# Residual rows turned on VectorE, x's features in a permuted order, decay's sums one piece later, vectors in one load

## The chip, the cores and the metric

The kernel runs on one core of one Trainium2 chip. The metric is the device time of one execution in microseconds. The times before are 1664.04, 1663.55 and 1665.42 us; their median is 1664.04 us.

## The reference

A hybrid of a Conformer layer and an mLSTM layer over 256 latent tokens (x) with a context prefix of 256 tokens (ctx), 1024 features, batch 1. All is fp32. Each sub-layer computes x <- LN(ALPHA*x + gate * F(x*(1+scale)+shift)), where scale, shift and gate come from a conditioning vector (adaLN). Cut to what matters here:

```python
for i in range(DEPTH):                       # DEPTH = 2
    sh1, sc1, g1, sh2, sc2, g2 = adaln(c, ada_w[i], ada_b[i])
    u = modulate(h, sh1, sc1)
    # layer 0: y = conformer_conv(u, ...); layer 1: y = mlstm_mixer(u, uc, ...)
    h = layer_norm(ALPHA * h + g1 * y, ln1_g[i], ln1_b[i])
    h = layer_norm(ALPHA * h + g2 * sq_relu_mlp(modulate(h, sh2, sc2), mlp_w1[i], mlp_w2[i]), ln2_g[i], ln2_b[i])
    # layer 0 does the same for the context tokens

# in the mLSTM: gates -> decay
lf = jax.nn.log_sigmoid(f_pre)
bcum = jnp.cumsum(lfc, axis=-1)              # running sums of the log forget gates, per head and direction
dlog = bcum[..., :, None] - bcum[..., None, :] + ic[..., None, :]
o = jax.nn.sigmoid(xm @ w_o + b_o)           # output gates
```

## The kernel before

The hidden state lies with features on the partitions: x is eight tiles of 128 features by 512 tokens (256 of the context, LO, then 256 latent, HI). A matrix product in fp32 is three passes of TensorE: each operand is split into a rounded high part (a cast by ScalarE, line 151) and a low rest (a subtraction by VectorE, line 152), and the products high-high, high-low and low-high add up in PSUM (`mm3`, lines 182 to 186, and `mm3t`, lines 213 to 215, where the roles of weights and data are exchanged). Weights come as 1 MB loads on SyncE's queue (`raw_load`, line 145, three buffers), and are split into `wh` and `wl`, four buffers each.

The order on each engine is not the order of the text alone. The framework's planner places each instruction when its inputs are due by its own costs; the place in the text decides between those that are due. `tc.issue_after` queues an instruction behind another one of its engine.

Stages that the change touches:

- The start. `vecs` holds all small vectors, 408 columns on 128 partitions. The first 64 columns (the two conditioning vectors and layer 0's adaLN bias) are loaded ahead of everything else (line 117), the other 344 after the loads of the second feature block (line 657). Then `start0` and `start1` run over eight feature blocks: one adaLN weight load, a load of x, a load of pw1 weights, matmuls (line 344).
- Between the products up_z and up_x of layer 1. The layer's input is also wanted as rows (tokens on the partitions) for the residual sum of layer 1. Eight ScalarE instructions (line 1199) scale the latent half of x; TensorE turns it in 16 transposes of 128x128 into PSUM (line 1202), ScalarE copies the result into the tile R (line 1204) and stores it to the DRAM tile `r_dr` (line 1205).
- The gate stage. Main work and side work are two chains of generators. The table `att` says which: first `['o0', 'G0 W0 T0 W1', 2]`, i.e. the output gates of head 0 (`gate_o`) with the side pieces `decay`, `weights(0)`, `guards`, `weights(1)`, two side pieces after each main piece; then `['o1', 'A0 W2', 1.6]`, and so on. A main piece of `gate_o` is 12 matmuls 512 wide; a head has 16 of them, eight for each direction d, and after each direction two adds read the sums out of PSUM (og, line 1588). `decay` brings the gates into columns (line 1398), takes log sigmoid (lines 1412 to 1421, two of them on ScalarE: Exp and Ln), makes running sums by matmuls with a triangle (lines 1435 and 1436, "decay's sums"), turns the result (line 1443), scans it and stores the negated row maxima `negm` to DRAM (`ng_dr`, line 1451). `weights(h)` loads rows of `ng_dr` spread over all partitions (line 1510) and builds the decay matrices from them on ScalarE and VectorE.
- The load of R from `r_dr` (line 1573), written ahead of the second half of head 0's gates, behind the latest weight load. R is first used by `down(0)`, beside the gates of head 2.

The tile R and the tiles that turn v (line 1261, VectorE transposes in 32x32 blocks, stored in four pieces at line 1265) share one buffer, "res".

Of the kernel before, what the change touches and what calls it, by code (L numbers as in the profile page):

```python
# [14 lines left out]
P = 128  # L15
D = 1024
DT = D // P
# [4 lines left out]
C = 256  # L22
# [34 lines left out]
_OFF = {}  # L57
# [14 lines left out]
def hybrid_kernel(ctx: ExitStack, tc: tile.TileContext, xT, vecs_d, wdw_d, ada0_w, ada_w, wg_d, pw1a, pw1, pw2, w1_0, w2_0,  # L72
                  w1_1, w2_1, up_x, up_z, wv, wo, bo_d, wk, wq, wqT, wdown, rows_d, out):
    nc = tc.nc
# [10 lines left out]
    def nm(s):  # L85
        uid[0] += 1
        return f"{s}_{uid[0]}"
# [3 lines left out]
    def tmp(tag, dt=F32):  # L91
        return tp.tile([P, T], dt, tag=tag, name=nm(tag), bufs={"E": 4, "S": 2, "L": 2, "F": 1}[tag])
# [8 lines left out]
    def psum(tag="mm"):  # L101
        return pp.tile([P, 512], F32, tag=tag, name=nm(tag), bufs={"mm": 3, "ln": 2, "fl": 1, "cv": 2}[tag])
# [10 lines left out]


    vecs = con.tile([P, NV], F32, name="vecs")
    NV0 = _OFF["ada_b1"][0]
    nc.sync.dma_start(vecs[:, :NV0], vecs_d[:, :NV0])

    def V(name, i=0, n=1):
        o = _OFF[name][0]  # L120
# [2 lines left out]
    def VA(name):  # L123
        o, w = _OFF[name]
        return vecs[:, o:o + w]

    ident = con.tile([P, P], F32, name="ident")
# [484 lines left out]
    x, u = [], []  # L612
# [41 lines left out]
    start1(0)  # L654
    idle(spare, 5)
    start0(1)
    nc.sync.dma_start(vecs[:, NV0:], vecs_d[:, NV0:])
    for f in range(DT):
        start2(f, (0,))
        if f + 1 < DT:  # L660
# [295 lines left out]
    cv = [psum("cv") for _ in range(2)]  # L956
# [234 lines left out]
    def rows_tile():  # L1191
        return xp.tile([P, 2, D], F32, tag="res", name=nm("res"), bufs=1)

    r_dr = dp.tile([P, 2, D], F32, name="r_dr")
    R = rows_tile()
    for f in range(0, DT, 2):
        t, tr = tmp("S"), psum("cv")
        for i in range(2):
            nc.scalar.activation(t[:, i * C:(i + 1) * C], x[f + i][:, HI], AF.Identity, scale=al[:, 0, f + i:f + i + 1],
                                 bias=al[:, 1, f + i:f + i + 1])  # L1200
            for tt in range(2):
                nc.tensor.transpose(tr[:, tt * C + i * P:tt * C + (i + 1) * P],
                                    t[:, i * C + tt * P:i * C + (tt + 1) * P], ident)
        nc.scalar.copy(R[:, :, f * P:(f + 2) * P], tr.rearrange("p (t c) -> p t c", t=2))
    nc.scalar.dma_start(r_dr, R)

    xm = []

# [99 lines left out]
    S = {}  # L1308
# [83 lines left out]
    def decay(_):  # L1392
        gT = tmp("L")
        nc.scalar.copy(gT, gps)
        yield
        gk = psum("ln")
        for b in range(4):
            nc.tensor.matmul(gk[:, b * 16:(b + 1) * 16], gT[:, b * P:(b + 1) * P], foldg, start=True, stop=True)
        gs = tmp("S")[:, 0:64].rearrange("p (b c) -> p b c", b=4)
        nc.vector.tensor_tensor(gs, gk[:, 0:64].rearrange("p (b c) -> p b c", b=4),  # L1400
                                VA("b_gate").rearrange("p (b c) -> p b c", b=4), op=ALU.add)
        gb_ = [tmp("L"), tmp("E"), tmp("E")]
        g8 = [gb_[i // 3][:, (i % 3) * 4 * NG:(i % 3 + 1) * 4 * NG].rearrange("p (b c) -> p b c", b=4) for i in range(8)]
        ig, fg, bsb, ex, up1, cor, lf, fa = g8
        nc.vector.memset(ig, 0.0)
        nc.vector.memset(fg, 0.0)
        for d in range(2):
            nc.vector.tensor_copy(ig[:, :, 32 * d:32 * d + 4], gs[:, :, 8 * d:8 * d + 4])
            nc.vector.tensor_copy(fg[:, :, 32 * d:32 * d + 4], gs[:, :, 8 * d + 4:8 * d + 8])


        nc.vector.scalar_tensor_tensor(fa, fg, -1.0, fg, op0=ALU.mult, op1=ALU.max)
        nc.scalar.activation(ex, fa, AF.Exp, scale=-1.0)
        nc.vector.tensor_scalar(up1, ex, 1.0, None, op0=ALU.add)
        nc.vector.scalar_tensor_tensor(cor, up1, -1.0, ex, op0=ALU.add, op1=ALU.subtract)
        nc.scalar.activation(lf, up1, AF.Ln)
        nc.vector.reciprocal(up1, up1)
        nc.vector.tensor_tensor(cor, cor, up1, op=ALU.mult)
        nc.vector.tensor_tensor(lf, cor, lf, op=ALU.subtract)
        nc.vector.tensor_scalar(fa, fg, 0.0, None, op0=ALU.min)  # L1420
        nc.vector.tensor_tensor(lf, lf, fa, op=ALU.add)

        nc.vector.memset(up1, 0.0)
        for d, (b0, b1, b2, b3) in ((0, (0, 1, 2, 3)), (1, (1, 0, 3, 2))):
            c = slice(32 * d, 32 if d == 0 else NG)
            nc.vector.tensor_copy(up1[:, b1, c], lf[:, b0, c])
            nc.vector.tensor_tensor(up1[:, b2, c], up1[:, b1, c], lf[:, b1, c], op=ALU.add)
            nc.vector.tensor_tensor(up1[:, b3, c], up1[:, b2, c], lf[:, b2, c], op=ALU.add)
        yield
        yield  # L1430
        bps = psum("ln")
        for d, cum in ((0, upper), (1, lower)):
            c = slice(32 * d, 32 if d == 0 else NG)
            reg = bps[:, 0:4 * NG].rearrange("p (b c) -> p b c", b=4)[:, :, c]
            nc.tensor.matmul(reg, cum, lf[:, :, c], start=True, stop=False)
            nc.tensor.matmul(reg, ones, up1[:, :, c], start=False, stop=True)
        nc.vector.tensor_copy(bsb, bps[:, 0:4 * NG].rearrange("p (b c) -> p b c", b=4))
        nc.vector.tensor_tensor(acol, ig, bsb, op=ALU.subtract)

        yield  # L1440
        aT = psum("ln")
        for b in range(4):
            nc.tensor.transpose(aT[:NG, b * P:(b + 1) * P], acol[:, b, :], ident)
        aR, mR = tmp("S"), tmp("S")
        nc.vector.tensor_copy(aR[:32, :], aT[:32, :])
        nc.vector.tensor_copy(aR[32:NG, LO], aT[32:NG, LO])
        nc.vector.tensor_copy(aR[32:NG, HI], aT[32:NG, T - 1:C - 1:-1])
        nc.vector.tensor_tensor_scan(mR[:NG, :], aR[:NG, :], aR[:NG, :], 0.0, op0=ALU.max, op1=ALU.max)
        nc.vector.tensor_scalar(negm[:32, :], mR[:32, HI], -1.0, None, op0=ALU.mult)
        nc.vector.tensor_scalar(negm[32:NG, :], mR[32:NG, T - 1:C - 1:-1], -1.0, None, op0=ALU.mult)  # L1450
        nc.scalar.dma_start(ng_dr, negm)
        bsbs.append(bsb)
        yield
# [42 lines left out]
    G1 = rows(qe.tile([P, D], F32, name="G1"), rows_d[0:1])  # L1496
    R = rows_tile()
    for i in range(2):
# [59 lines left out]
    for i in range(2):  # L1558
        rx = raw_load(xl_dr[i].rearrange("p b c -> p (b c)"))
        for j in range(8):  # L1560
            t = XL(F32R)
# [4 lines left out]
    def gate_o(h):  # L1566

        for d in range(2):
            bo = rows(BO().rearrange("p a b -> p (a b)"), bo_d[h:h + 1, d * DH:(d + 1) * DH])
            pss = [psum() for _ in range(2)]  # L1570
            if (h, d) == (0, 1):
                with tc.issue_after(loaded[0]):
                    nc.sync.dma_start(R, r_dr)
            for q in range(4):
                ws = preo if (h, d, q) == (0, 0, 0) else None
                if ws is None:
                    raw = raw_load(wo[h, d, q])
                for i in range(2):
                    w = ws[i] if ws else split_w(raw[:, i * 1024:(i + 1) * 1024])
                    for t in range(2):  # L1580
                        for k in range(2):
                            kt = 4 * q + 2 * i + k
                            sl = slice(k * 512, (k + 1) * 512)
                            mm3t(pss[t], xls[kt][0][:, BLK[t]], xls[kt][1][:, BLK[t]], w[0][:, sl], w[1][:, sl],
                                 kt == 0, kt == ET - 1)
                        if q == 3 and i == 1:
                            og[h, d, t] = o_ = OG()
                            nc.vector.tensor_tensor(o_, pss[t], bo, op=ALU.add)  # L1588
                            nc.scalar.activation(o_, o_, AF.Sigmoid)
                    yield  # L1590
# [73 lines left out]
    def down(h):  # L1664
# [18 lines left out]
        if h == 0:  # L1683
            for hf, ws in enumerate(load()):
                for t in range(2):
# [3 lines left out]
                    nc.vector.tensor_tensor(e_, ps, G1[:, HF[hf]], op=ALU.mult)  # L1689
                    nc.vector.tensor_tensor(R[:, t, HF[hf]], R[:, t, HF[hf]], e_, op=ALU.add)  # L1690
                    yield
# [28 lines left out]
    def residual(t, hf, ps, G):  # L1720

        e_ = tmp("E")
        nc.vector.tensor_tensor(e_, ps, G[:, HF[hf]], op=ALU.mult)
        nc.vector.tensor_tensor(R[:, t, HF[hf]], R[:, t, HF[hf]], e_, op=ALU.add)
        if hf == 0:
# [240 lines left out]
def _layout(np, i):  # L1966
    g = {k: np.asarray(v) for k, v in i.items()}
    a, turned = {}, _turned(np)
    a["xT"] = np.concatenate([g["ctx"][0], g["x"][0]], axis=0).T
    vec = {  # L1970
        "c_ctx": _cols(g["c_ctx"]), "c": _cols(g["c"][0]),
        "b_pw1": _cols(g["conv_b_pw1"][0]),
# [32 lines left out]
    a["wqT"] = g["ml_w_q"][0].T.reshape(ET, P, E)  # L2005
    a["wdown"] = g["ml_w_down"][0].reshape(H, 4, P, 2, 512).transpose(0, 3, 2, 1, 4).reshape(H, 2, P, 2048)
    a["w2_1"] = g["mlp_w2"][1].reshape(16, 2, P, D).transpose(0, 2, 1, 3).reshape(16, P, 2048)
    ab = g["ada_b"][1].reshape(6, D)
    a["rows_d"] = np.stack([ab[2], ab[5], g["ln1_g"][1], g["ln1_b"][1], g["ln2_g"][1], g["ln2_b"][1]])
    return {k: np.ascontiguousarray(v) for k, v in a.items()}  # L2010

# [22 lines left out]
```

## Time and profile before

| | |
|---|---|
| median of 3 runs | 1664.04 us (1663.55 to 1665.42) |
| profiled execution, own time | 1665.14 us |
| its span, first to last instruction | 1663.4 us |
| TensorE busy | 1648.7 us, 99% |
| VectorE busy | 1038.1 us, 62% |
| ScalarE busy | 734.6 us, 44% |
| DMA | 303.70 MB, mean 183 GB/s |
| granted TensorE clock | 0.999 |

The profile is of one execution on the chip. PE is TensorE's matmuls, PEld its weight loads, DVE is VectorE, ACT ScalarE, POOL GpSimd, SP SyncE; ACTq and SPq are rows of the queues that issue DMAs. A row of a timeline has start and duration in us, engine, line, operation, output <- input, shape and count, and in brackets the idle time of the engine ahead of it with what ended it. A row of a line has minimum, median and maximum duration in ns.

### The profile page before, as it was taken

What the parts mean: (1) busy time and instruction counts of PE and PEld (TensorE: products, weight loads), DVE (VectorE), ACT (ScalarE), POOL (GpSimd) and SP (SyncE); (2) the same over time, 40 slices, a digit from 0 to 9 for tenths busy, and PEclk for the clock granted to TensorE, in tenths of its full rate; (3) what the DMA queues carried; (4) which work ended last, traced back from release to release, by engine and by line L of the source; (5) the groups of instructions that cost most, each with busy time, mean ns of one, the idle gap of its engine ahead of it and who ended that gap; (6) DMA issues with size and microseconds to landing.
All of it is one profiled execution on the core that took longest, in us unless ns stands there. A gap on an engine that the chain in (4) does not pass through costs nothing.

```text
span 1663.4 us, 22731 instructions
## 1 busy us (share of the span) xinstructions
PE 1648.7 (99%) x8856; PEld 1357.6 (82%) x8856; DVE 1038.1 (62%) x1863; ACT 734.6 (44%) x1182; POOL 14.4 (1%) x64
## 2 busy tenths in 40 slices
PE   9999999999999999999999999999999999999998
PEld 6665898888888998877787899888877888878886
DVE  6554895666535765762354753553489876776677
ACT  4313573232324476652233533442477654555453
POOL 0000000000000000000000000000000000000001
PEclk9999999999999999999999999999999999999999
DMA  9555223534324065557774852554465555675552
GB/s 353 208 210 214 92 75 111 167 123 148 136 101 152 4 228 194 184 196 266 278 259 146 302 179 79 179 194 144 148 240 197 203 215 203 250 284 183 178 194 85
DMA packets 74331, 303.70 MB, mean 183 GB/s; under 512 B 7694, under 2 KB 23858, under 8 KB 44144
## 3 DMA queue, kind: packets, MB, share of 16 engines
q1 hardware_dynamic: 56368, 286.49, 49.1%
q10 hardware_dynamic: 17856, 15.77, 2.8%
q8 instruction: 69, 1.13, 0.3%
q14 instruction: 38, 0.31, 0.1%
HBM read 285.42 MB, written 16.81 MB: 182 GB/s over the span
## 4 chain that ended last, share of the span: by engine, by line
PE 95%; DVE 2%; DMA 1%; ACT 1%; issue 0%; SPq 0%; DVEq 0%; ACTq 0%
PE mm L182 18%; PE mm L185 17%; PE mm L186 17%; PE mm L197 7%; PE mm L198 4%; PE mm L215 3%; PE mm L213 3%; PE mm L214 3%; PE cv L213 2%; PE cv L215 2%; PE cv L214 2%; PE fl L344 1%; PE ln L182 1%; PE cv L860 1%; PE ln L214 1%; PE ln L185 1%
## 5 line engine op out<-in xcount | busy, mean ns | idle before, releaser
L152 DVE TENSOR_TENSOR wl<-raw,wh 128x1024 fp32r<-128x1024 f32 x344 | 418.7, 1221 | 245.5 <-ACT wh L151 233.4
L151 ACT CAST wh<-raw 128x1024 fp32r<-128x1024 f32 x344 | 358.6, 1051 | 469.3 <-PE mm L185 244.4
L185 PE MATMUL mm<-u,wh 128*128 128x512 f32 (+1 forms) x808 | 291.5, 361 | 0.2 <-DVE u L604 0.2
L182 PE MATMUL mm<-u,wh 128*128 128x512 f32 (+1 forms) x680 | 243.8, 359 | 0.0
L186 PE MATMUL mm<-u,wl 128*128 128x512 f32 (+1 forms) x680 | 241.3, 355 | 0.0
L185 PEld LDWEIGHTS mm<-u,wh 128*128 128x128 f32 x808 | 152.7, 189 | 23.2 <-issue 1.0
L182 PEld LDWEIGHTS mm<-u,wh 128*128 128x128 f32 x680 | 128.4, 189 | 24.4 <-issue 6.3
L186 PEld LDWEIGHTS mm<-u,wl 128*128 128x128 f32 x680 | 128.5, 189 | 17.8
L213 PE MATMUL mm<-wh,xl 128*128 128x512 f32 x256 | 101.0, 395 | 0.7 <-DVE og L1588 0.7
L182 PE MATMUL mm<-xm,wh 128*128 128x512 f32 x256 | 101.0, 394 | 0.0
L215 PE MATMUL mm<-wl,xl 128*128 128x512 f32 x256 | 100.0, 393 | 0.0
L214 PE MATMUL mm<-wh,xl 128*128 128x512 f32 x256 | 99.9, 390 | 0.0
L186 PE MATMUL mm<-xm,wl 128*128 128x512 f32 x256 | 99.7, 389 | 0.0
L182 PE MATMUL mm<-hid,wh 128*128 128x512 f32 (+1 forms) x256 | 93.3, 364 | 0.0
L186 PE MATMUL mm<-hid,wl 128*128 128x512 f32 (+1 forms) x256 | 92.8, 363 | 0.0
L185 PE MATMUL mm<-hid,wh 128*128 128x512 f32 (+1 forms) x256 | 92.8, 363 | 0.0
L197 PE MATMUL mm<-x,wh 128*128 128x512 f32 x232 | 81.1, 398 | 0.0
L185 PE MATMUL mm<-qq,wh 128*128 128x272 f32 x256 | 73.9, 289 | 0.0
L182 PE MATMUL mm<-qq,wh 128*128 128x272 f32 x256 | 73.5, 288 | 0.0
L186 PE MATMUL mm<-qq,wl 128*128 128x272 f32 x256 | 73.5, 288 | 0.0
L197 PE MATMUL mm<-u,wh 128*128 128x512 f32 x192 | 68.6, 399 | 0.0
L1099 DVE SCALAR_TENSOR_TENSOR x<-mm,ada,x 128x256 f32<-128x256 f32 x64 | 28.5, 479 | 63.4 <-PE mm L186 63.4
(537 smaller groups left out, 3249.4 us busy)
## 6 DMA issues: line engine op xcount, KB each, us to landing
raw<-w SPq DMA_DIRECT2D x64, 1024.0 KB, 4.9
raw<-wo SPq DMA_DIRECT2D x32, 1024.0 KB, 4.9
raw<-ada_w SPq DMA_DIRECT2D x22, 1024.0 KB, 7.0
ar<-ada_w SPq DMA_DIRECT2D x80, 256.0 KB, 3.9
raw<-wv SPq DMA_DIRECT2D x16, 1024.0 KB, 8.0
raw<-wqT SPq DMA_DIRECT2D x16, 1024.0 KB, 5.7
raw<-wq SPq DMA_DIRECT2D x16, 1024.0 KB, 5.8
raw<-wk SPq DMA_DIRECT2D x16, 1024.0 KB, 5.2
```

The costliest lines, as they stand in the source:

```text
L151: c = nc.scalar.copy(hi, src)
L152: lastsub[0] = nc.vector.tensor_tensor(lo, src, hi.bitcast(F32), op=ALU.subtract).ins
L182: a = nc.tensor.matmul(ps, wh, xh, start=start, stop=False)
L185: nc.tensor.matmul(ps, wh, xl, start=False, stop=False)
L186: lastmm[0] = nc.tensor.matmul(ps, wl, xh, start=False, stop=stop).ins
L197: todo = [lambda s_, e_: nc.tensor.matmul(ps, wh, r[0], start=s_, stop=e_), lambda s_, e_: nc.tensor.matmul(ps[:, :n], wl, r[0][:, :n], st ...
L198: lambda s_, e_: nc.tensor.matmul(ps[:, :n], wl, r[0][:, :n], start=s_, stop=e_)]
L213: nc.tensor.matmul(ps, xh, wh, start=start, stop=False)
L214: nc.tensor.matmul(ps, xl, wh, start=False, stop=False)
L215: nc.tensor.matmul(ps, xh, wl, start=False, stop=stop)
L344: a = mark_unit[0] = nc.tensor.matmul(ps[32 * j:32 * j + 32], cs[:, kt, 14 - 2 * v:46 - 2 * v], blocks[kt], start=first and kt < 4, stop=l ...
L1099: nc.vector.scalar_tensor_tensor(res[m][:, sl_], p_, g[:, m:m + 1], res[m][:, sl_], op0=ALU.mult, op1=ALU.add)
```

## The change

Four edits. (1) The residual rows are turned by VectorE: eight transposes of 128x256 in 32x32 blocks write straight from the scaled x into the "res" tile, and four stores on ScalarE's queue, one for each 32 partitions, put the rows into `r_dr`. Such a turn exchanges rows and columns inside each block and leaves a block on its 32 partitions, so x's features are held in a permuted order through layer 0 and up to up_x (partition 32r+i of tile f holds feature 256r+32f+i): each store then writes 256 neighbouring features of all rows. The arrays of weights and vectors are permuted to match when they are laid out before the launch. The 16 transposes on TensorE and the four copies out of PSUM are gone. (2) `decay` has one more empty `yield` ahead of its sums. (3) The load of R is written one head later, in the second half of head 1's gates. (4) `vecs` is loaded by one DMA at the start.

```diff
--- before.py
+++ after.py
@@ -113,8 +113,7 @@
 
 
     vecs = con.tile([P, NV], F32, name="vecs")
-    NV0 = _OFF["ada_b1"][0]
-    nc.sync.dma_start(vecs[:, :NV0], vecs_d[:, :NV0])
+    nc.sync.dma_start(vecs, vecs_d)
 
     def V(name, i=0, n=1):
         o = _OFF[name][0]
@@ -654,7 +653,6 @@
     start1(0)
     idle(spare, 5)
     start0(1)
-    nc.sync.dma_start(vecs[:, NV0:], vecs_d[:, NV0:])
     for f in range(DT):
         start2(f, (0,))
         if f + 1 < DT:
@@ -1192,17 +1190,16 @@
         return xp.tile([P, 2, D], F32, tag="res", name=nm("res"), bufs=1)
 
     r_dr = dp.tile([P, 2, D], F32, name="r_dr")
-    R = rows_tile()
+    vr = rows_tile().rearrange("p a (b m j) -> p a b m j", m=DT, j=32)
     for f in range(0, DT, 2):
-        t, tr = tmp("S"), psum("cv")
+        t = tmp("S")
         for i in range(2):
             nc.scalar.activation(t[:, i * C:(i + 1) * C], x[f + i][:, HI], AF.Identity, scale=al[:, 0, f + i:f + i + 1],
                                  bias=al[:, 1, f + i:f + i + 1])
-            for tt in range(2):
-                nc.tensor.transpose(tr[:, tt * C + i * P:tt * C + (i + 1) * P],
-                                    t[:, i * C + tt * P:i * C + (tt + 1) * P], ident)
-        nc.scalar.copy(R[:, :, f * P:(f + 2) * P], tr.rearrange("p (t c) -> p t c", t=2))
-    nc.scalar.dma_start(r_dr, R)
+            nc.vector.transpose(vr[:, :, :, f + i, :], t[:, i * C:(i + 1) * C])
+    for r in range(4):
+        nc.scalar.dma_start(r_dr[:, :, r * C:(r + 1) * C].rearrange("(q j) t x -> j t q x", j=32),
+                            vr[32 * r:32 * r + 32].rearrange("j t q m i -> j t q (m i)"))
 
     xm = []
 
@@ -1426,6 +1423,7 @@
             nc.vector.tensor_copy(up1[:, b1, c], lf[:, b0, c])
             nc.vector.tensor_tensor(up1[:, b2, c], up1[:, b1, c], lf[:, b1, c], op=ALU.add)
             nc.vector.tensor_tensor(up1[:, b3, c], up1[:, b2, c], lf[:, b2, c], op=ALU.add)
+        yield
         yield
         yield
         bps = psum("ln")
@@ -1568,7 +1566,7 @@
         for d in range(2):
             bo = rows(BO().rearrange("p a b -> p (a b)"), bo_d[h:h + 1, d * DH:(d + 1) * DH])
             pss = [psum() for _ in range(2)]
-            if (h, d) == (0, 1):
+            if (h, d) == (1, 1):
                 with tc.issue_after(loaded[0]):
                     nc.sync.dma_start(R, r_dr)
             for q in range(4):
@@ -1966,7 +1964,16 @@
 def _layout(np, i):
     g = {k: np.asarray(v) for k, v in i.items()}
     a, turned = {}, _turned(np)
-    a["xT"] = np.concatenate([g["ctx"][0], g["x"][0]], axis=0).T
+    xs = np.arange(D).reshape(4, DT, 32).transpose(1, 0, 2).reshape(D)
+    for n in ("conv_w_pw1", "mlp_w1", "ml_w_up"):
+        g[n] = np.concatenate([g[n][:1][:, xs], g[n][1:]])
+    for n in ("conv_w_pw2", "mlp_w2", "conv_b_pw2", "ln1_g", "ln1_b", "ln2_g", "ln2_b"):
+        g[n] = np.concatenate([g[n][:1][..., xs], g[n][1:]])
+    ab = g["ada_b"][1].reshape(6, D)
+    for n in ("ada_w", "ada_b"):
+        t = g[n].reshape(2, -1, 6, D)
+        g[n] = np.concatenate([t[:1][..., xs], np.concatenate([t[1:, :, :2][..., xs], t[1:, :, 2:]], axis=2)]).reshape(g[n].shape)
+    a["xT"] = np.concatenate([g["ctx"][0], g["x"][0]], axis=0).T[xs]
     vec = {
         "c_ctx": _cols(g["c_ctx"]), "c": _cols(g["c"][0]),
         "b_pw1": _cols(g["conv_b_pw1"][0]),
@@ -2005,7 +2012,6 @@
     a["wqT"] = g["ml_w_q"][0].T.reshape(ET, P, E)
     a["wdown"] = g["ml_w_down"][0].reshape(H, 4, P, 2, 512).transpose(0, 3, 2, 1, 4).reshape(H, 2, P, 2048)
     a["w2_1"] = g["mlp_w2"][1].reshape(16, 2, P, D).transpose(0, 2, 1, 3).reshape(16, P, 2048)
-    ab = g["ada_b"][1].reshape(6, D)
     a["rows_d"] = np.stack([ab[2], ab[5], g["ln1_g"][1], g["ln1_b"][1], g["ln2_g"][1], g["ln2_b"][1]])
     return {k: np.ascontiguousarray(v) for k, v in a.items()}
```

## The prediction

> **What bounds the kernel now.** I read the page first: engine shares, then the chain that ended last.
>
> ```profile
> span 1663.4 us, 22731 instructions
> PE 1648.7 (99%) x8856; PEld 1357.6 (82%) x8856; DVE 1038.1 (62%) x1863; ACT 734.6 (44%) x1182; POOL 14.4 (1%) x64
> PE 95%; DVE 2%; DMA 1%; ACT 1%; issue 0%; SPq 0%; DVEq 0%; ACTq 0%
> ```
>
> TensorE is the chain. An edit moves the end in two ways only: it changes how long TensorE's own stream is, or it changes a wait of TensorE. So the next view is the waits of TensorE alone; these are the longest, in us in total, times, and longest.
>
> ```profile
> PE ln L1435 <- DVE E L1421: 1.6, 1, 1.6
> PE fl L344 <- DMA raw<-ada_w: 1.4, 2, 1.2
> ...
> PE mm L213 <- DVE og L1588: 0.7, 1, 0.7
> ```
>
> The change touches all three: the first load stands ahead of the ada_w load (second row), and decay's sums are L1435 (first row); the third comes later in the same stage. The sum is made on the profiled execution: span 1663.4 us, its own time 1665.14. The median of the runs shown is 1664.04, 1.10 lower, and I subtract the same microseconds from it. A measurement of this kernel can tell about 0.2% from no change: 3.3 us.
>
> **Part 1, the residual rows.** Removed from TensorE: 16 transposes, L1202. The timeline of TensorE where up_z ends and up_x begins (start, duration):
>
> ```profile
> 628.95 0.28 PE L186 MATMUL mm<-u,wl 128*128 128x256 f32 x1
> 629.07 1.04 PE L1202 MATMUL cv<-ident,S 128*128 128x128 f32 x8
> 629.86 0.47 PE L182 MATMUL mm<-u,wh 128*128 128x512 f32 x1
> 630.17 0.39 PE L185 MATMUL mm<-u,wh 128*128 128x512 f32 x1
> 630.40 0.39 PE L186 MATMUL mm<-u,wl 128*128 128x512 f32 x1
> ...
> 632.23 0.39 PE L185 MATMUL mm<-u,wh 128*128 128x512 f32 x1
> 632.47 0.38 PE L1202 MATMUL cv<-ident,S 128*128 128x128 f32 x2
> ...
> 634.28 0.40 PE L182 MATMUL mm<-u,wh 128*128 128x512 f32 x1
> ```
>
> Durations overlap, so I count from start to start. A 256-wide matmul takes 0.12 (628.95 to 629.07), a 512-wide one 0.23 (630.17 to 630.40). The first eight transposes hold the stream from 629.07 to 629.86, 0.79, and the matmul behind them takes 0.31 instead of 0.23: 0.87 together. From 632.23 to 634.28 stand five matmuls and the other eight transposes in four pairs: 2.05 - 5 x 0.23 = 0.90. TensorE never waits in this stretch, so its stream gets 1.77 us shorter, and that is the one gain that follows from the rows alone.
>
> What takes their place lies on other engines. Here are the stage by engine, ScalarE's evacuations that go, the nearest VectorE transpose and the nearest store of turned rows (both of v), and ScalarE's next wait:
>
> ```profile
> 599.00:636.00 37.00, 37.00 (x291) 35.95 (x291) 18.49 (x20) 27.87 (x48) 0.00 (x0) 1.00 0.78 273
> L1204 ACT COPY res<-cv x4: 579/586/587, 630.4 to 634.3; 128x512 f32<-128x512 f32 x4
> L1261 DVE STREAM_TRANSPOSE res<-vt x16: 702/706/714, 735.1 to 914.9; 128x512 f32<-128x512 f32 x16
> L1265 ACTq DMA_DIRECT2D v_dr<-res x16: 577/674/2011, 769.4 to 917.7; - x16
> 636.53 0.59 ACT L1217 COPY pad<-mm 128x512 f32<-128x512 f32 x1 [1.70 <-PE mm L186]
> ```
>
> The window's columns are length, then busy time of PE, PEld, DVE, ACT and POOL. VectorE gets eight transposes of 128x256. Half of 0.706 to the whole of it bounds one: 2.8 to 5.6 us; I take 0.40 each, near the half, 3.2 us. VectorE has 18.5 idle in these 37 us and nobody on TensorE's side waits for the rows: cost 0. ScalarE loses 4 x 0.586 = 2.3 us of copies and one store, and gets four stores: at 0.577 to 2.011 each, 2.3 to 8.0 us of its queue; I take the median, 4 x 0.674 = 2.7. That is even. Queued behind a store that waits for the last VectorE transpose are the evacuations of up_z and the casts of up_x's weights. ScalarE waits 1.70 for TensorE at 636.53 and is idle 9 of the 37 us, so I take 0; if that cover is gone the price is in the third rival. The store's runs get shorter, its bytes are the same 1 MB. The permuted order of x's features adds no instruction: the arrays are laid out so before the launch.
>
> [...]
>
> **Part 2, vectors in one load.** The first load grows by the second's size.
>
> ```profile
> vecs<-vecs_d SPq DMA_DIRECT2D x1, 172.0 KB, 7.9
> 2.50:3.00 0.50, 0.50 (x5) 0.50 (x4) 0.00 (x0) 0.49 (x1) 0.50 (x4) 1.00 0.00 0
> 3.50:4.00 0.50, 0.50 (x4) 0.50 (x4) 0.00 (x0) 0.49 (x2) 0.00 (x0) 1.00 0.93 393
> ```
>
> At the 393 GB/s of the last row 172 KB take 0.45 us, ahead of the ada_w load for which TensorE waits 1.2. But the last two columns (share of the DMA engines, GB/s) show nothing moving from 2.50 to 3.00: a hole of 0.5 between the small load and ada_w. So 0 if it fills the hole, 0.45 if it doesn't; I take 0.1. The second ada_w load has the same bytes more ahead of it, but the same hole. Leaving the second issue out frees SP of one issue; no wait of TensorE hangs on it.
>
> **Part 3, decay's sums.** The side chain takes two pieces after each main piece of gate_o, a main piece being 12 matmuls (four each at L213, L214 and L215). The sums are piece 4, written after 8 of each; the new yield makes them piece 5, after 12. The transposes of acol, the scan, the store of negm and the row loads of `weights` also go one piece back. But where are they now? Here are a group of TensorE's from the first gate matmul to the sums, and rows of ScalarE, VectorE and TensorE from the timeline:
>
> ```profile
> L213 PE MATMUL mm<-wh,xl 128*128 128x512 f32 x23 | 9.5, 411 | 0.0
> ```
>
> ```profile
> 1207.03 2.00 ACT L151 CAST wh<-raw 128x1024 fp32r<-128x1024 f32 x2 [3.21 <-DMA raw<-wo]
> 1209.05 1.28 ACT L1413 ACT_TABLE_LOAD   x1
> ...
> 1214.25 1.19 DVE L152 TENSOR_TENSOR wl<-raw,wh 128x1024 fp32r<-128x1024 f32 x1
> ...
> 1214.39 0.39 PE L214 MATMUL mm<-wh,xl 128*128 128x512 f32 x1
> 1216.40 0.49 PE L1435 MATMUL ln<-E,tri 128*128 128x128 f32 x2 [1.63 <-DVE E L1421]
> ```
>
> The sums run after 23, not after 8: they were planned for when their data would be there, not for their written place. A written place of 12 is still far ahead of 23. Their data is late because the exponential stands behind two casts that waited 3.21 us for wo, and because a 1.19 split stands ahead of the last VectorE steps. The yield touches neither. So I take 0 for this wait. Its bounds: 1.63 gained if the plan puts 12 more matmuls (12 x 0.23 = 2.76 us) ahead of the sums; 1.1 lost if it does so and everything that hangs on the sums comes 2.76 - 1.63 later.
>
> What hangs on them is a round trip through memory and a solid stretch of VectorE (its window, then the timeline):
>
> ```profile
> 1231.90:1249.30 17.40, 16.73 (x73) 12.97 (x72) 17.37 (x42) 15.20 (x31) 0.00 (x0) 1.00 0.58 213
> ```
>
> ```profile
> 1231.93 0.48 DVE L1525 SCALAR_TENSOR_TENSOR S<-L,acol,mask 128x256 f32<-128x256 f32 x1 [2.53 <-DMA L<-ng_dr]
> ...
> 1248.22 0.41 DVE L1539 TENSOR_TENSOR F<-F,S 128x256 f32<-128x256 f32 x1
> 1248.55 0.67 DVE L1588 TENSOR_TENSOR og<-mm,bo 128x512 f32<-128x512 f32 x1
> ...
> 1249.28 0.50 PE L213 MATMUL mm<-wh,xl 128*128 128x512 f32 x1 [0.67 <-DVE og L1588]
> ```
>
> VectorE is busy 17.37 of 17.40 us from the landing of ng_dr's rows to the og add for which TensorE waits 0.67. So the first wait's gain can be lost here: if that wait goes and the landing stays, TensorE comes 1.63 sooner to an add that is no sooner. The half step also moves pieces of `weights(1)` back; each operation like the one at 1248.22 that falls behind the og add brings the add 0.41 nearer. Bounds 0 and 0.67; I take 0.3 gained, the middle, since one such operation is about what half a piece moves.
>
> **Part 4, the residual load moved.** The R load leaves o0 for o1 on SP's queue, past the ng_dr, v_dr, zs_dr, bo and wo loads.
>
> ```profile
> 1204.49 0.43 SPq L1573 DMA_DIRECT2D res<-r_dr  x1
> ...
> 1274.78 1.05 ACT L151 CAST wh<-raw 128x1024 fp32r<-128x1024 f32 x1 [3.36 <-DMA raw<-wo]
> ```
>
> The wo load that made the casts wait until 1207.03 was ahead of the issue at 1204.49, so taking it away there gains 0. In o1 the casts wait 3.36 for wo without TensorE waiting; another 1 MB (2.7 us at 393 GB/s) hides behind the weights already cast: 0, or 2.7 if they run out.
>
> **Sum.** -1.77 + 0.1 + 0 - 0.3 + 0 = -2.0: 1662.0, which is within 0.2%. By its bounds this case runs from 1661.6 (first load 0, the whole 0.67) to 1663.9 (first load 0.45, nothing at the og add, 1.1 lost at the sums).
>
> **The rivals.** *Both waits go.* The plan does leave 12 matmuls ahead of the sums and the og add comes ahead of `weights(1)`: -1.77 - 1.63 - 0.67 + 0.1 = -4.0, 1660.0. For: the wait is 1.63 and a main piece 2.8. Against: 23 matmuls, not 8, and VectorE's solid stretch.
>
> *The round trip comes later (slower).* The sums go 1.1 later, and the ng_dr row loads come on SP's queue behind a wo load: 1 MB is 2.7 more. VectorE's stretch has no slack, so the og add is 3.8 later, TensorE with it: -1.77 + 0.1 + 3.8 = +2.1, 1666.2; if the second head's rows come behind a load too, 2.7 more, 1668.8. It decides from a landing 1.7 later on. For: casts wait for wo in both stages (3.21, 3.36), so its loads are in flight there all the time. Against: the row loads go out when the store of negm has landed, which a half step alone moves little.
>
> *The turn is dearer off TensorE.* ScalarE is held 8.0 us by four stores inside up_z, where a PSUM bank of three comes round after two groups of 24 matmuls at 0.12 (24 x 0.12 x 2 = 5.8): TensorE waits 2.2, and -1.77 + 0.1 + 2.2 = +0.5 gives 1664.6; if two of the three banks are caught, twice that wait, 1666.8. Issued later than 629, beside matmuls of 0.23, it costs nothing. For: a store of v's rows has taken 2.011. Against: the median of 0.674 and the idle ScalarE. [...]
>
> *The yield does nothing at all* is the forecast itself with 0 for the second wait: 1662.3.
>
> **How the numbers follow.** Forecast 0.40, which holds the case that the yield does nothing; both waits go 0.36; round trip later 0.18, two thirds of it with the larger price; dearer turn 0.06, half of it together with a late round trip. Faster by over 0.2% (below 1660.7) is the first rival and 0.03 of the forecast (sums' wait gone, most of it kept): 0.39. Slower by over 0.2% (above 1667.4) is 0.12 of the round trip and 0.03 of the dearer turn: 0.15. Within: 0.46. The range goes from 1659.5 (first rival, less another 0.5 that the R load's absence could free in front of the sums) to 1666.2 (the round trip's smaller price); what lies above it is the 0.15. The likeliest case alone: 1661.6 to 1663.9.
>
> **What would show it.** No TensorE row between 629 and 634 other than L182, L185, L186; eight VectorE transposes near 0.40; ScalarE's store rows under 1 us each. TensorE's wait at the sums: 1.6 means the yield moved nothing; gone, with a larger wait at the og add, that the second kept the books; both gone, the first rival. ng_dr's rows landing over 1.7 later than 1231.9 is the slower rival. TensorE's wait for ada_w, 1.4 in all before, prices the first load. A wait of TensorE for wh or wl in o1 would make part 4 wrong.

## The result and the profile after

| | before | after |
|---|---|---|
| median | 1664.53 us (20 runs, 1662.74 to 1666.54) | 1666.82 us (20 runs, 1664.57 to 1672.22) |
| ratio | | 1.0017, 95% interval 1.0011 to 1.0023 |
| profiled execution, own time | 1665.14 us | 1666.15 us |
| its span | 1663.4 us | 1664.4 us |

The changed kernel is slower by 0.17%, where 1662.0 us had been forecast. The executions of one kernel spread over 3.8 us (before) and 7.7 us (after), so times below are ratios of runs on one chip, and single executions are compared stretch by stretch.

In the page after, TensorE still is the chain, with the 16 transposes gone (8856 to 8840 matmuls). It is no less busy, though, and the page alone does not tell why.

```profile
span 1664.4 us, 22701 instructions
PE 1648.8 (99%) x8840; PEld 1357.2 (82%) x8840; DVE 1040.2 (62%) x1871; ACT 732.6 (44%) x1178; POOL 14.3 (1%) x64
PE 96%; DVE 2%; DMA 0%; ACT 0%; issue 0%; SPq 0%; DVEq 0%; ACTq 0%
```

The view that tells it is the waits of TensorE (us in total, times, longest). Three of its lines answer to the three of before: the wait for ada_w is 1.3 after 1.4, the one at decay's sums (now L1433) 0.7 after 1.6, the one for og is gone. The first line is new, and larger than all that went.

```profile
PE mm L181 <- ACT wh L150: 3.1, 2, 2.8
PE fl L343 <- DMA raw<-ada_w: 1.3, 2, 1.0
...
PE ln L1433 <- DVE E L1418: 0.7, 1, 0.7
```

The timeline of TensorE shows where it stands: behind the first group of up_x. (Lines have moved: 181, 184 and 185 are before's 182, 185 and 186.)

```profile
628.94 0.40 PE L181 MATMUL mm<-u,wh 128*128 128x512 f32 x1
...
634.18 0.39 PE L185 MATMUL mm<-u,wl 128*128 128x512 f32 x1
637.40 0.50 PE L181 MATMUL mm<-u,wh 128*128 128x512 f32 x1 [2.83 <-ACT wh L150]
637.74 0.40 PE L184 MATMUL mm<-u,wh 128*128 128x512 f32 x1
638.36 0.50 PE L181 MATMUL mm<-u,wh 128*128 128x512 f32 x1 [0.22 <-ACT wh L150]
638.69 0.40 PE L184 MATMUL mm<-u,wh 128*128 128x512 f32 x1
639.18 0.74 PE L185 MATMUL mm<-u,wl 128*128 128x512 f32 x1
...
641.00 0.63 PE L181 MATMUL mm<-u,wh 128*128 128x512 f32 x1
641.42 0.63 PE L184 MATMUL mm<-u,wh 128*128 128x512 f32 x1
...
642.70 0.39 PE L184 MATMUL mm<-u,wh 128*128 128x512 f32 x1
...
721.62 0.39 PE L181 MATMUL mm<-xm,wh 128*128 128x512 f32 x1
```

No transpose stands in it any more, and nothing but the three matmul lines, as forecast. But TensorE waits 2.83 and 0.22 us for a cast weight, and then starts a matmul every 0.42 us (641.00 to 641.42) instead of every 0.23, until 642.70. The windows of this stretch give the granted clock, where 1.00 is TensorE at its full speed (the three last columns are granted clock, share of the DMA engines and GB/s):

```profile
637.40:639.10 1.70, 1.47 (x4) 0.59 (x4) 1.70 (x3) 1.70 (x2) 0.00 (x0) 1.00 0.00 0
639.10:642.50 3.40, 3.32 (x8) 2.65 (x9) 3.40 (x5) 1.73 (x3) 0.14 (x2) 0.52 0.67 224
642.50:646.00 3.50, 3.50 (x16) 2.82 (x16) 1.35 (x2) 0.62 (x2) 0.00 (x0) 0.97 1.03 209
```

The clock was 0.52 for 3.4 us behind the wait. Eight starts from 639.18 to 642.70 took 3.52 us; at before's 0.227 (45 starts from 639.73 to 649.93 there) they take 1.82, so the clock cost 1.7.

Why the cast was late stands in ScalarE's timeline, which carries both the casts (L150) and the stores of the rows (L1201):

```profile
624.16 1.05 ACT L150 CAST wh<-raw 128x1024 fp32r<-128x1024 f32 x1
624.76 0.70 ACTq L1201 DMA_DIRECT2D r_dr<-res  x1
626.26 0.38 ACT L1178 ACTIVATE E<-mm 128x256 f32<-128x256 f32 x1 [1.05 <-PE mm L185]
629.14 0.38 ACT L1178 ACTIVATE E<-mm 128x256 f32<-128x256 f32 x1 [2.50 <-PE mm L185]
...
630.01 3.46 ACTq L1201 DMA_DIRECT2D r_dr<-res  x3
634.61 0.59 ACT L1214 COPY pad<-mm 128x512 f32<-128x512 f32 x1 [5.08 <-PE mm L185]
...
636.32 3.87 ACT L150 CAST wh<-raw 128x1024 fp32r<-128x1024 f32 x4
```

Before, four casts of up_x's weights (there L151) stood ahead of the first copy out of up_x's PSUM (there L1217, at 636.53):

```profile
621.41 1.05 ACT L151 CAST wh<-raw 128x1024 fp32r<-128x1024 f32 x1
...
623.39 1.05 ACT L151 CAST wh<-raw 128x1024 fp32r<-128x1024 f32 x1 [0.93 <-PE mm L185]
...
626.27 1.05 ACT L151 CAST wh<-raw 128x1024 fp32r<-128x1024 f32 x1 [1.55 <-PE mm L185]
...
629.15 1.05 ACT L151 CAST wh<-raw 128x1024 fp32r<-128x1024 f32 x1 [1.55 <-PE mm L185]
```

Now there is one, then four stores, then L1214, which cannot start before TensorE has finished up_x's first group at 634.6, and the next four casts only behind that. TensorE uses up the one cast block and waits for ScalarE, which had been waiting for TensorE. The weights were not late: the third up_x load was issued at 620.2, the loads issued from 612 to 640 landed at most 5.3 us after their issue, so it was there by 625.6, and the casts began at 636.32.

A measure that is free of what happens elsewhere is the time from up_x's first 512-wide matmul to the first matmul on `xm` (628.94 to 721.62 above): 92.68 us, where before it was 88.07 (629.86 to 717.93). I call it the up_x stretch.

### The profile page after: what moved, and what is told of

The parts are those of the page before. It is cut to its first block, busy times and chain, and to the rows that moved or that the text cites. A ratio compares the mean times of both kernels' runs of the same rounds, so it can differ in the third digit from the quotient of the medians.

```text
span 1664.4 us, 22701 instructions
## 1 busy us (share of the span) xinstructions
PE 1648.8 (99%) x8840; PEld 1357.2 (82%) x8840; DVE 1040.2 (62%) x1871; ACT 732.6 (44%) x1178; POOL 14.3 (1%) x64
## 4 chain that ended last, share of the span: by engine, by line
PE 96%; DVE 2%; DMA 0%; ACT 0%; issue 0%; SPq 0%; DVEq 0%; ACTq 0%
PE mm L181 18%; PE mm L184 17%; PE mm L185 17%; PE mm L196 7%; PE mm L212 4%; PE mm L214 4%; PE mm L213 4%; PE mm L197 4%; PE cv L212 2%; PE cv L214 2%; PE cv L213 2%; PE fl L343 1%; PE ln L181 1%; PE cv L858 1%; PE ln L184 1%; PE fl L765 1%
## 5 line engine op out<-in xcount | busy, mean ns | idle before, releaser
L151 DVE TENSOR_TENSOR wl<-raw,wh 128x1024 fp32r<-128x1024 f32 x344 | 418.8, 1222 | 249.8 <-ACT wh L150 247.5
L150 ACT CAST wh<-raw 128x1024 fp32r<-128x1024 f32 x344 | 358.3, 1050 | 476.6 <-PE mm L184 250.2
```

The costliest lines, as they stand in the source:

```text
L150: c = nc.scalar.copy(hi, src)
L151: lastsub[0] = nc.vector.tensor_tensor(lo, src, hi.bitcast(F32), op=ALU.subtract).ins
```

## The experiments

Theory: the loss is the order on ScalarE's queue (three of up_x's first four casts behind the stores and behind the copy that waits for TensorE), 3.05 us of wait, and the low clock behind it. Rivals: A, the loss comes from the other three edits; B, the short runs of the four stores hold up the DMA engines; C, the gate stage's smaller waits exist only because TensorE came there later; D, the low clock has a cause of its own. All ratios are to the kernel before on the same chip; they come from the single runs and are not exactly the quotient of the two medians beside them (for the kernel without the yield that would be 0.9980). The last column is the rest of the profiled execution, from the first matmul on `xm` to the end of the span. It is 945.5 and 944.2 in two executions of the kernel before, and 942.8 in the changed kernel.

| kernel | median us | before us | ratio (95%) | up_x stretch us | rest us |
|---|---|---|---|---|---|
| rows alone | 1667.87 | 1664.64 | 1.0017 (1.0008 to 1.0026) | 92.24 | 946.6 |
| all but the rows | 1664.77 | 1664.64 | 1.0004 (0.9995 to 1.0013) | 88.08 | 943.8 |
| stores on SyncE's queue | 1660.48 | 1664.64 | 0.9976 (0.9967 to 0.9985) | 87.07 | 942.3 |
| stores later on ScalarE | 1661.17 | 1664.64 | 0.9980 (0.9971 to 0.9988) | 87.07 | 943.9 |
| 40 filler matmuls | 1668.50 | 1664.18 | 1.0026 (1.0015 to 1.0037) | 95.39 | 942.7 |
| 14 filler matmuls | 1666.51 | 1664.58 | 1.0011 (1.0002 to 1.0019) | 91.07 | 944.4 |
| rows alone, stores on SyncE | 1661.92 | 1664.18 | 0.9987 (0.9978 to 0.9996) | 87.07 | 945.6 |
| stores on SyncE, no yield | 1660.88 | 1664.18 | 0.9985 (0.9976 to 0.9994) | 87.07 | 943.2 |
| stores on SyncE, R early | 1662.86 | 1664.18 | 0.9991 (0.9982 to 1.0000) | 87.07 | 945.8 |
| stores on SyncE, vectors in two | 1660.50 | 1664.58 | 0.9976 (0.9966 to 0.9987) | 87.07 | 943.4 |

**Rows alone** (kernel before with edit 1).

```diff
-    nc.sync.dma_start(vecs, vecs_d)
+    nc.sync.dma_start(vecs[:, :NV0], vecs_d[:, :NV0])
...
-        yield
...
-            if (h, d) == (1, 1):
+            if (h, d) == (0, 1):
```

> Kernel before with edit 1 alone: the rows turned on VectorE and the four stores on ScalarE's queue; vectors in two loads, the sums and the load of R as before. Theory (the four stores are queued on ScalarE ahead of three of up_x's four first weight casts; TensorE runs out of weights in up_x's first group, 2.8 + 0.2 us, and then runs about 2 us longer at a lower granted clock): the loss is all here, -1.7 for the transposes and +5.4 in the first group of up_x, so +3.7 us against before, ratio 1.002, and the two waits 'PE mm <- ACT wh' of the changed kernel stand in the profile near 637 and 638; the wait for the sums stays at 1.6 and that for og at 0.7. Rival A (the loss comes from the gate stage or the start, edits 2 to 4): this kernel is 1.7 faster than before, ratio 0.999. Rival B (the shorter runs of the stores hold up the DMA engines, and the weights land later): like the theory in time, but the casts themselves wait for raw.

The ratio is that of the whole change, 1.0017. The waits of TensorE show the same pair, beside a wait at the sums that is no smaller than before's:

```profile
PE mm L182 <- ACT wh L151: 3.0, 2, 2.8
PE ln L1434 <- DVE E L1420: 1.9, 1, 1.9
```

Rival A falls: edit 1 alone brings the loss.

**All but the rows** (the changed kernel with before's TensorE transposes and feature order).

```diff
-            nc.vector.transpose(vr[:, :, :, f + i, :], t[:, i * C:(i + 1) * C])
+            for tt in range(2):
+                nc.tensor.transpose(...)
+        nc.scalar.copy(R[:, :, f * P:(f + 2) * P], ...)
```

> The changed kernel with edit 1 undone: residual rows turned on TensorE as before, x's features in their natural order; vectors in one load, the sums one piece later, the load of R one head later. Theory (the loss sits in edit 1 alone): the start gives 0.1 and the gate stage about 1.8 (sums' wait 1.6 to 0.7, og wait 0.7 to 0, 0.2 elsewhere), so -1.9 us against before, ratio 0.9989; no wait for wh at 637. Rival A (edits 2 to 4 lose): 1 to 3 us slower than before, ratio over 1.0005. Rival C (the gate stage's gain in the changed kernel exists only because TensorE came there 3.7 us later): 0 us, ratio 1.0000, waits of 1.6 and 0.7 as before.

The stretch is before's and no wait for wh at 637 is there, so the loss is gone with the rows. My -1.9 for the other edits was a miss: +0.1 in the medians, the interval reaching from -0.8 to +2.2 us. It was read from one execution's waits; what those are worth is shown by the repeat below. The waits at the sums and for og are 0.5 and 0.4 here, not the 1.6 and 0.7 of rival C.

**Stores on SyncE's queue**, and **stores later on ScalarE** (written later, inside up_x): both keep the rows and the four stores, and move only their place.

```diff
-        nc.scalar.dma_start(r_dr[:, :, r * C:(r + 1) * C]...
+        nc.sync.dma_start(r_dr[:, :, r * C:(r + 1) * C]...
```

> The changed kernel with its four stores of the rows issued on SyncE's queue instead of ScalarE's; nothing else is changed. Theory (what costs is the place of the stores on ScalarE's queue): up_x's first four casts stand ahead of the first read of PSUM again, the waits for wh at 637 and the low clock behind them go, 5.4 us come back: -3.6 us against before, ratio 0.9978. Rival B (short runs and DMA traffic of the same four stores): the loss stays, +2 against before, and the casts wait for raw; the stores then also stand in front of weight loads on SyncE's queue, so it could be larger. Rival A: no change from the changed kernel, +2.

```diff
-    for r in range(4):
-        nc.scalar.dma_start(r_dr[...], vr[...])
-    gemm(up_x, range(8), ...)
+    for i, _ in enumerate(gemm_steps(up_x, range(8), ...)):
+        if i in (3, 5, 7, 9):
...
+            nc.scalar.dma_start(r_dr[...], vr[...])
```

> The changed kernel with its four stores of the rows still on ScalarE's queue, but written one by one inside up_x, after its steps 3, 5, 7 and 9; nothing else is changed. Theory: the casts of up_x's weights are ahead of the stores again, so the wait for wh and the low clock go: -3.6 us against before, ratio 0.9978, as with the other queue. Rival B (DMA traffic of the short runs): the loss moves with the stores by some us and stays, +2 against before. If this one gains and the one on SyncE's queue doesn't, the stores in front of the weight loads cost there.

Both came out as the theory had it, 0.9976 and 0.9980 against 0.9978, and both beat both kernels. ScalarE's timeline of the kernel with the stores on SyncE:

```profile
623.82 2.00 ACT L150 CAST wh<-raw 128x1024 fp32r<-128x1024 f32 x2
...
626.20 1.04 ACT L150 CAST wh<-raw 128x1024 fp32r<-128x1024 f32 x1
...
628.68 1.05 ACT L150 CAST wh<-raw 128x1024 fp32r<-128x1024 f32 x1 [1.44 <-PE mm L184]
...
634.04 1.05 ACT L150 CAST wh<-raw 128x1024 fp32r<-128x1024 f32 x1 [4.03 <-PE mm L184]
634.99 0.58 ACT L1214 COPY pad<-mm 128x512 f32<-128x512 f32 x1
```

Five casts stand ahead of L1214, and the up_x stretch is 87.07: 1.00 less than before's 88.07, where the transposes in it were priced at 0.90 and the slow matmul at its start at 0.08. The same stores in the same short runs go out at 624.4 to 627.7, and no wait of TensorE for a weight is in that trace, so B falls. With the stores written later ScalarE still issues them (607 to 826 ns each). By the planner's order two of them still go out before the first copy, here L1211, but with four casts ahead of it (two at 623.75, and the two below):

```profile
626.13 1.04 ACT L150 CAST wh<-raw 128x1024 fp32r<-128x1024 f32 x1
...
626.63 0.70 ACTq L1231 DMA_DIRECT2D r_dr<-res  x1
...
629.01 1.04 ACT L150 CAST wh<-raw 128x1024 fp32r<-128x1024 f32 x1
...
629.51 0.61 ACTq L1231 DMA_DIRECT2D r_dr<-res  x1
634.20 0.59 ACT L1211 COPY pad<-mm 128x512 f32<-128x512 f32 x1 [4.14 <-PE mm L185]
```

So it is the order of casts and copy that counts, not which engine issues the stores. Nor is it how long they hold the queue: in the changed kernel they were done at 633.47, before the copy could start at 634.61, and in the kernel with 14 fillers below they took 0.58 to 0.69 each with the casts as late.

**Fillers** (the changed kernel, and 40 or 14 idle matmuls of ones behind up_x's first group).

```diff
-    gemm(up_x, range(8), ...)
+    for i, _ in enumerate(gemm_steps(up_x, range(8), ...)):
+        if i == 0:
+            idle(psum("cv"), 40)
```

> The changed kernel with 40 matmuls of ones (128x128, into a spare PSUM bank, their result unused) written behind up_x's first group, where TensorE waits 2.83 us for wh; the stores and casts stay on ScalarE. It adds work that the reference does not have. Theory (the wait itself costs 3.05 us, and the clock of 0.52 behind it another 2 because TensorE was idle): the wait is filled by 2 to 2.6 us of matmuls, the granted clock between 639 and 643 stays at 1.0, so about 2 us less than the changed kernel, ratio to before 1.0003 to 1.0008. Rival D (the low clock there comes from something else, power for instance): clock 0.5 as before, time as of the changed kernel or longer, ratio 1.0015 to 1.003.

> As the kernel with 40 matmuls of ones behind up_x's first group, but with 14, sized by that run: 40 held TensorE from 634.50 to 642.68, 0.204 us each, so 14 take 2.9 us, about the 2.83 us that TensorE waits for wh there. The work of 14 is extra and its result unused. Theory (an idle TensorE loses its clock): the wait is filled, the granted clock behind it stays 1.0, so 2 to 2.4 us less than the changed kernel: ratio to before 1.0002 to 1.0007. Rival D (the clock falls there for another reason): no gain, ratio 1.0015 or more.

The 40 were mis-sized: they ran 8.2 us, five more than the wait, and the kernel got slower. The 14 nearly fit: two waits for wh are left, of 0.38 and 0.21 us. Their windows, of the kernel with 14:

```profile
637.40:639.10 1.70, 1.11 (x5) 0.53 (x4) 1.66 (x3) 1.70 (x3) 0.00 (x0) 1.00 0.00 0
639.10:642.50 3.40, 3.31 (x14) 2.42 (x14) 3.40 (x5) 1.99 (x3) 0.14 (x2) 1.00 0.53 157
```

The casts are as late as ever (four from 636.84, behind L1214), but the clock stays at 1.00 where it had been 0.52, and the stretch is 1.6 us shorter than the changed kernel's (92.68 to 91.07), less than the 2 to 2.4 expected and near the 1.7 worked out above. With 40 it stayed at 1.00 as well. So D falls: it was TensorE's standing still that cost the clock here. The ratios point the same way, but 1.0011 lies between what was expected (1.0007 at most) and what D was to give (1.0015), and its interval overlaps that of 1.0017; the traces decide here.

**Rows alone, stores on SyncE** (edit 1 with the queue changed, edits 2 to 4 undone).

> Kernel before with edit 1 alone, its four stores on SyncE's queue: no late sums, no moved load, vectors in two loads. If the rows are worth what TensorE's timeline says (16 transposes, 1.77 us) and the three other edits nothing (as the kernel without the rows measured, ratio 1.0004), then -1.8 against before, ratio 0.9989, and the version with all four edits and the stores on SyncE, measured at 0.9976, owes its other 2 us to the other edits only where the rows are turned off TensorE. If the rows alone give all 4 us, ratio 0.9976, then the removed transposes are worth more than their place in the stream. Waits at the sums near 1.6 and at og near 0.7 are expected to stay.

-2.2 us in the ratio (-3.7 to -0.7): the transposes' 1.77 fits. The wait at the sums is 1.5, as expected; the one for og is gone, which was not.

**The other edits one by one**, each undone in the kernel with its stores on SyncE: without the yield, with the load of R back at (0, 1), with the vectors in two loads.

> The version with the stores on SyncE's queue (0.9976) with the yield ahead of decay's sums taken out again. If the later sums are worth something: a wait at the sums of about 1.6 returns and the ratio is 0.9986 (1.6 us slower than with the yield). If the yield does nothing in the mean, as my forecast had it for this wait: 0.9976.

> The version with the stores on SyncE's queue (0.9976) with the load of R back in the second half of head 0's gates. If that load holds up a weight load there: a wait for wh or a later landing of ng_dr's rows, 0.5 to 2.7 us, ratio 0.9979 to 0.9992. If it is hidden, as my forecast had it: 0.9976 and no wait that names raw or wh in the gate stage.

> The version with the stores on SyncE's queue (0.9976) with vectors loaded in two parts again. My forecast had the single load at 0.1 us lost (0 to 0.45): so 0.9976 and the wait for ada_w between 0.2 and 1.4 in both, as its size has differed between the profiles of kernels whose start is the same. If the one load is worth something of its own: 0.9980 or more.

Two loads of the vectors measure the same as one; TensorE waits for ada_w in neither, where 0.2 to 1.4 was expected. The yield is unclear in the ratios: the intervals of 0.9985 and 0.9976 overlap, and the wait at the sums came back as 0.6, not 1.6. The early load of R is 0.9991, about 2.5 us behind 0.9976, with intervals that overlap a little. Its waits of TensorE in that stage:

```profile
1213.53 0.49 PE L1433 MATMUL ln<-E,tri 128*128 128x128 f32 x2 [0.98 <-DVE E L1418]
1245.74 0.50 PE L214 MATMUL mm<-wl,xl 128*128 128x512 f32 x1 [1.31 <-DVE wl L151]
1247.61 0.50 PE L212 MATMUL mm<-wh,xl 128*128 128x512 f32 x1 [0.68 <-DVE og L1586]
```

In the trace of the kernel with the stores on SyncE and the load late, none of the three is there. The longest goes back to a load by way of two queues (ScalarE's and VectorE's timelines):

```profile
1241.17 1.05 ACT L150 CAST wh<-raw 128x1024 fp32r<-128x1024 f32 x1 [2.08 <-DMA raw<-v_dr]
...
1242.66 0.83 DVE L1526 TENSOR_TENSOR S<-S,x 128x256 f32<-128x256 f32 x2 [1.77 <-ACT S L1519]
...
1244.47 1.22 DVE L151 TENSOR_TENSOR wl<-raw,wh 128x1024 fp32r<-128x1024 f32 x1
```

The v_dr load goes out at 1233.87 (with the load of R late at 1229.39) and lands 7.2 us later; a cast waits for it; VectorE waits for the ScalarE work behind that cast; and behind that on VectorE stands the split of wo's weights for which TensorE waits until 1245.74. This is read from one trace; why the v_dr load goes out later was not isolated.

That the early load costs something does not hang on one trace. The last column of the table sorts itself by this edit, but for an overlap of 0.2 us: 944.2 to 946.6 us in the five traces with the load early (those of before among them), 942.3 to 944.4 in the eight with it late, 2.2 us apart in the mean. The waits of TensorE account for 1.3 of them. The place of the sums sorts the same way: 68 matmuls of gate_o stand ahead of them in each of the five and 73 in each of the eight, with the yield or without. So the yield moved nothing, and the load's move put the sums five matmuls (5 x 0.227 = 1.14 us; 34 starts from 1206.68 to 1214.39 in before) later. Rival C falls too: the four kernels with late load and a gain (0.9976 to 0.9985) reach the first `xm` matmul at 715.6 to 716.0, sooner than before (717.9), and have the short rest all the same.

Why all but the rows, also with the load late, is no faster than before in its runs stays open. In its trace the rest is 1.7 us shorter than in before's first, and 1.6 us are lost near 60 us to a low clock (last section); whether other executions of that kernel lose them too is not known.

**Before once more**, unchanged.

> The kernel before, unchanged, in a second profiled execution. If TensorE's short waits are fixed by the program: 1.6 at the sums, 1.4 for ada_w, 0.7 for og again, each within 0.2. If they come from when the loads land in one execution, they come out otherwise by some tenths to more than 1 us, and then they can't be read as prices of the edits from one profile.

```profile
PE mm L213 <- DVE og L1588: 0.7, 1, 0.7
...
PE ln L1435 <- DVE E L1421: 0.5, 1, 0.5
```

The wait at the sums is 0.5 here and was 1.6, in the same program; the wait for ada_w (1.4) is not in the list at all. Between the first `xm` matmul and the sums this execution took 497.35 us, the other 498.47: it is the 1.1 us of that wait. So a wait of this size in one execution is not a price. The wait at the sums shows that in the other traces as well: it is 1.8 us with the stores later on ScalarE and absent with them on SyncE, at ratios of 0.9980 and 0.9976.

## Why the prediction was wrong

**Part 1, the transposes: right.** TensorE's offset to before goes from -0.12 at 33.7 us to -0.92 at up_x's first matmul, and the stretch behind it loses another 1.00 once nothing waits: 1.8, where 0.87 + 0.90 was forecast.

**Part 1, what takes their place: the step that failed.** The sizes were near: VectorE's transposes took 403/445/447 ns (0.40 taken), ScalarE's stores 0.70 and 3.46 together, 4.2 (2.7 taken, up to 8.0 allowed), though one of them took 1.85, where under 1 each was to be seen. The step was "Queued behind a store that waits for the last VectorE transpose are the evacuations of up_z and the casts of up_x's weights. ScalarE waits 1.70 for TensorE at 636.53 and is idle 9 of the 37 us, so I take 0". The names were right and the conclusion wrong: the cover was not ScalarE's idle time but four casts done ahead of the first copy out of up_x, and the new order on the queue took three of them away. The idle time ahead of the copy that waited for TensorE was of no use to the casts queued behind it: ScalarE did no work for 5.08 us just there (the issue of three stores, 3.46, lies inside them), and the casts came only after, at 636.32. The price was 92.68 - 87.07 = 5.6 us: 3.05 of waits, 1.7 of clock, the rest slower starts around the waits (0.34 from 637.40 to 637.74, 0.49 from 638.69 to 639.18).

**The dearer turn** (chance 0.06) had the right queue and the wrong place. It priced a PSUM bank in up_z, where TensorE has no wait in the list after, and said that a store later than 629 costs nothing; the three stores at 630.01 are in the order that cost most. The VectorE turn with the stores elsewhere is faster: 0.9987 with edit 1 alone and the stores on SyncE.

**Part 2:** 0.1 forecast, none measured; the ada_w wait was 1.3.

**Part 3:** the yield moved nothing, as forecast, but the sums did move: 73 matmuls of gate_o instead of 68 stand between the first of them and the sums in the changed kernel (25 of the first kind instead of 23), and they came with edit 3. The wait that I left standing at 1.63 was 0.68 after, and 0.5 in the repeat of before. What failed is to take one execution's wait as a constant. ng_dr's rows were first used at 1236.79, 4.86 later than before. By the letter of the forecast's sign (over 1.7 later than 1231.9) that is the slower rival; but TensorE itself came 3.67 later to the first gate matmul and the sums 3.87 later, so the round trip grew by only 1.0, and TensorE does not wait for the og add that this rival had 3.8 later. VectorE has no more slack than before (17.19 of 17.41 us busy from 1236.79 on); the first og add comes 14.25 us after the first use of the rows, where it came 16.62 after it. The og wait went, as in the forecast's upper bound. With the stores on SyncE's queue neither wait is in the trace and the median is 1660.48, near the first rival's 1660.0, but not by its cause: by the table it is the load's move that counts, not the yield.

**Part 4, a second step that failed:** no wait for wh or wl stands in o1 in the changed kernel, as forecast. But "so taking it away there gains 0" was wrong: the load's move is worth about 2.2 us of the rest (945.5 to 943.3 in the mean). One row, the wait for wo until 1207.03, was taken for all that the load could hold up.

The sum on the profiled execution: span +1.0, made of -0.9 ahead of up_x, +4.6 in its stretch and about -2.7 behind it, of which the two waits in the gate stage are 1.6. The medians are 2.3 apart, not 1.0; single executions of one kernel differ by that much, the last part alone by 1.3 between the two of before. With the mean of all traces for the load of R the terms are -1.8 for the transposes, +5.6 for the casts and -2.2 for the load: +1.6.

## What to carry to other kernels

When an engine's queue gets new entries, ask which producers for the bottleneck stand behind them, and whether an entry between them waits for the bottleneck itself: busy shares and idle time cannot show that, the order of the queue does. A DMA store takes time on its issuer's queue (0.59 to 1.85 us each on ScalarE's in the changed kernel, 0.59 to 1.23 on SyncE's); choose the queue whose next entries nobody waits for. And take a second profile of the unchanged kernel before pricing a wait of 1 us; a long stretch, compared over all the traces at hand, told more here than any single wait.

## What the runs showed of the hardware

A wait of 2.83 us, one more of 0.22 and little work between were followed by a granted clock of 0.52 for 3.4 us, so the stall cost over half as much again (1.7 after 3.05). With 14 fillers in the wait (0.38 and 0.21 us of it left) the clock in the same window was 1.00. How long a wait has to be to cost the clock no run here shows.

A shorter wait was followed by a low clock in some traces. At about 57.5 us four 31-row matmuls (1.95 us in before, the changed kernel and the kernel without the rows) stand behind a wait, which is 0.6 us in every trace. In three of the eleven traces whose clock was read there it fell behind them: in the kernel without the rows and in the two with the rows alone (0.57, 0.69 and 0.57 from 60 to 64 us). The first window below is of the kernel without the rows, the second of before:

```profile
60.00:62.00 2.00, 2.00 (x6) 1.58 (x5) 0.09 (x1) 1.17 (x2) 0.00 (x0) 0.51 0.52 147
```

```profile
60.00:62.00 2.00, 2.00 (x10) 1.62 (x9) 0.00 (x0) 0.65 (x1) 0.00 (x0) 1.00 0.45 115
```

Six matmuls run in place of ten in 2 us. The kernel without the rows was 0.46 us ahead of before at 59.24 and 1.18 behind at up_x's first matmul, 1.6 us lost. Up to there its program is that of the changed kernel, whose clock stayed at 1.00; what makes the difference is not known.

A store of 256 KB from 32 partitions held its queue 587, 668 (median) and 1848 ns, the single 1 MB store of before 326: four stores were not four times one.
